# A decoder trunk whose hand-ordered mixer gets other starting points for its pairs of heads and other handicaps for its threads

## The chip, the cores and the metric

The kernel runs on one core of one Trainium2 chip. The metric is the device time of one execution in microseconds (us). Views of the profile speak of the engines as PE (TensorE's matmuls), PEld (TensorE loading the stationary operand), DVE (VectorE), ACT (ScalarE), POOL (GpSimd) and SP (SyncE, which here only issues transfers).

## The reference

Two layers run over one sequence of 256 positions with 1024 channels. Each layer does, in float32:

```
x = x + 0.5 * swiglu_ffn(x, ffn1)                 # 1024 -> 2 x 2816 -> 1024
h = rms_norm(x);  z = h @ w_in                    # columns shared out among all branches and gates
o_sb  = stick_breaking_attention(...)             # 8 heads of 64
o_mla = mla_attention(...)                        # 8 heads, low-rank q and kv, rotary part of 32
o_nsa = nsa_attention(...)                        # 8 heads, 2 kv groups: compressed, selected, window
y = sum over the 3 branches of sigmoid(gate_b(h)) * (o_b @ proj_b)
x = x + y @ w_out
x = x + 0.5 * swiglu_ffn(x, ffn2)
```

The part from `h` to `x + y @ w_out` is the mixer. Its three attentions are small (256 queries, 256 keys); nearly all its arithmetic is products with weights.

## The kernel before

**The weight stream.** All weights are read once, in the order of use, as slabs of 128 rows by (mostly) 1024 columns. Each float32 slab is split into a high part (a copy on ACT, L926 in the mixer, L527 in the FFNs) and a low part (a subtraction on DVE, L928, L528), and each product is three matmuls: high by high, low by high, high by low (`mm3`, L573 to L575). A slab of 1024 columns is so 12 matmuls of 512 columns over the two halves of the sequence. Some of the mixer's slabs are split ahead of time during an FFN and parked in HBM (`split_early`; `EARLY_AT` says which, the first tuple for both layers, the second for layer 1 alone). These come back as two finished halves (L914) and need no ACT and no DVE work, but twice the bytes.

**The mixer's slabs** are numbered 0 to 68: 0 to 3 low-rank inputs, gates and rotary key, 4 to 7 the queries of the stick-breaking attention (SB), 8 to 14 its keys together with the MLA up-projections, 15 to 18 its values, 19 to 22 queries and 23 to 26 keys of the sparse attention (NSA), 27 to 30 a merge gate, 31 and 32 values of NSA, 33 to 34 the projection of SB, then gates and projections by turns with the compression weights of NSA at 39, 40 and 44, 45; 49, 50 and 55, 56 are the projection of MLA, 57 to 64 NSA's two merge gates, 65 to 68 NSA's projection, which needs the outputs of NSA's pairs of heads.

**The planner.** In the mixer the orders of PE, ACT and DVE are written out by a planner in the program: every strand of work is a generator (a thread) that yields one step at a time with its engine, its estimated duration, what it waits for and which buffers it needs. At each turn the planner issues the step with the lowest rank,

```
s = self.start(req[0], req[3], req[4])
rank = s + (th[0]() if callable(th[0]) else th[0]) + (0.5 * req[1] if isinstance(th[2], list) else 0.0)
```

where `s` is the earliest start by its own estimates in us and `th[0]` is the thread's handicap, `HOLDS`. The threads in the order of `HOLDS` are `hT_rest, tables, sb_T, sb_scores, sb_pv, cmp_in, nsa_prep, gates, mla_T, mla_scores, mla_P, mla_pv, nsa_T, k_chain, v_chain, cmp_scores, nsa_scores, nsa_P, nsa_pv, bulk`. `bulk` (handicap 0.3) is the weight products, slab after slab, which fill the time between the others. The thread that splits the weights has a handicap that depends on its lead over the slab in use (`URGENCY`: no slab of lead, one, two and more). The engines then run these orders as they stand: where a step is ready later than the planner estimated, its engine stands at it, whatever stands behind.

**The pairs.** Heads are worked on in pairs, four in each attention. A pair's first step waits for a gate, the end of a given slab:

```
def gate(at, p, ahead=0):
    return ev_used[max(0, at[p] + ahead)]
```

For SB the pair's transposes (L1353) wait for slab `SB_AT[p] - 2` and its scores (L1368, L1374) for `SB_AT[p]`; for MLA the same with `MLA_AT` (transposes L1521, scores at lines 573 to 575 into `att`); for NSA the scores (L1845) of pair `p` wait for slab `NSA_AT[2 * p]`, and the odd entries are not read. After the scores, `t_softmax` runs minima (DVE L1462), exponentials (ACT L1452), a reciprocal and a scaling (ACT L1484 or DVE L1482); `t_probs` transposes the result on PE (L1493) and splits it (ACT L944 or DVE L946, DVE L1501); PE multiplies by the values (MLA L1333 to L1339; NSA L1868 to L1871 twice for a pair and L1878, L1879 for the compressed branch); `put_o` adds two halves and splits the sum (ACT L1312, DVE L1318, ACT L952, DVE L954). SB has a longer chain in `sb_head` (L1382 to L1412, with two PE steps L1401, L1402 in the middle). Buffers that two pairs share: four `qk` tiles (a pair of SB takes two, of MLA all four, until its scores are done), four banks for scores (an SB or MLA pair takes two, an NSA pair all four), four `wf` and four `wr` tiles.

**The one transfer inside the mixer that PE waits for** is `zc`: POOL sends two tiles from `wf` to `zc` (L1216), and `cmp_in` transposes them (L1613).

Of the kernel before, what the change touches and what calls it, by code (L numbers as in the profile page):

```python
# [242 lines left out]
class Planner:  # L243
# [11 lines left out]
    def spawn(self, gen, hold=0.0):  # L255
        try:
            self.live.append([hold, gen, next(gen)])
        except StopIteration:
            pass
# [74 lines left out]
def use_t(count, *deps, slots=()):  # L334

    o = 0.2 + count * 0.109
    return "P", o, o + 0.2, deps, slots
# [15 lines left out]
TAIL = 3  # L353

MIX_SLABS = 69
SB_AT = 19, 21, 23, 26
MLA_AT = 30, 33, 36, 39

EARLY_AT = tuple(range(27, 47, 2)), tuple(range(28, 48, 2))

URGENCY = (-1.0, -0.3, 0.15)
HOLDS = (0.0, 2.0, 0.0, 0.0, 0.0, 0.05, 0.05, 0.05, 0.05, 0.05, 0.05, 0.05, 0.05, 0.05, 0.05, 0.0, 0.05, 0.05, 0.05, 0.3)
NSA_AT = 46, 48, 50, 52, 54, 56, 58, 60


@with_exitstack
def decoder_trunk(ctx, tc, x_in, wts, gains, lcon, cst, out, depth=DEPTH):
# [15 lines left out]
    def tp_tile():  # L383
        return pb.tile([128, 512], F, tag="ps", name="tp")
# [156 lines left out]
    def split_early(fp, l, part):  # L541

        for a in EARLY_AT[part]:
            i = l * len(plan) + FFN_SLABS + a
# [293 lines left out]
    def mixer(l):  # L838
# [98 lines left out]
        def urgency():  # L937
            return URGENCY[min(loading[0] - use_at[0], 2)]

# [408 lines left out]
        def sb_T():  # L1348
            for p in range(4):
                k = yield use_t(4, *ev_sbqk[0], *ev_sbqk[1], gate(SB_AT, p, -2), slots=(s_tp, s_qk, s_qk))  # L1350
                tp = tp_tile()
# [10 lines left out]
        def sb_scores():  # L1362
            for p in range(4):
                k = yield "P", 1.0, 1.2, (ev_qsb[p], gate(SB_AT, p)), (s_att, s_att)
                q = qsb[p]
# [70 lines left out]
        def gate(at, p, ahead=0):  # L1436

            return ev_used[max(0, at[p] + ahead)]
# [73 lines left out]
        def mla_T():  # L1512
            for p in range(4):
                T = []
                for i, (src, ev) in enumerate(((mq, ev_mq), (mk, ev_mk))):
                    k = yield use_t(4, *ev, gate(MLA_AT, p, -2), slots=(s_tp, s_qk, s_qk))
                    tp = tp_tile()
# [14 lines left out]
        def mla_scores():  # L1532
            for p in range(4):
                k = yield "P", 1.44, 1.64, (*ev_Tm[p], gate(MLA_AT, p), ev_tanh), (s_att, s_att)
                T = Tm[p]
                s = [att_tile() for _ in range(2)]
                r = slice(0, 96)
                for j in range(2):
                    o = 256 * j
                    mm3(s[j][:, 0:128], cut(T[0], r, slice(o, o + 128)), cut(T[1], r, slice(o, o + 128)),  # L1540
                        start=True, stop=True)
                    mm3(s[j][:, 128:384], cut(T[0], r, slice(o + 128, o + 256)), cut(T[1], r, slice(o, o + 256)),
                        start=True, stop=True)
                s_qk.put(k, k, k, k)
                sb = [(x[:, 0:128], x[:, 128:384]) for x in s]
                spawn(t_softmax(sb, 1.0 / math.sqrt(96.0), None, k, 0.01 * p, Em[p], ev_Em[p]), 0.01 * p)

        def mla_P():
            for p in range(4):
                yield from t_probs(Em[p], ev_Em[p], Pm[p], ev_Pm[p], 0.01 * p)  # L1550

        def mla_pv():
            for p in range(4):
                k = yield *PV, (*ev_Pm[p], *ev_V1), (s_acc,)
                oT = acc_tile()
                pv(oT, V1, (2 * p, 2 * p + 1), [[q[:, j] for q in Pm[p]] for j in range(2)])
                s_wr.put(k, k)
                spawn(put_o(o_mla, p, oT, k, ev_omla), 0.01 * p)
# [204 lines left out]
        def v_chain():  # L1763

            k = yield use_p(64, 3, ev_hidT[1], slots=(s_acc,))
            a = acc_tile()
            mm3(a[:, 0:64], flat(hvs[1]), cut(tab["w2"], A, slice(64, 128)), start=True, stop=True)
            vs = mp.tile([128, 2, 64], R, name="vc")
            k = yield from t_split(vs[:, 0], vs[:, 1], a[:, 0:64], 64, k)
            s_acc.put(k)  # L1770
            k = yield use_v(1024, k)
            nc.vector.tensor_tensor(Vc, bc(vs.rearrange("p a d -> p (a d)"), 8),
                                    cc("vm")[:, :, None].to_broadcast([128, 8, 128]), op=OP.mult)
            ev_vc.set(k)
# [59 lines left out]
        def nsa_scores():  # L1834

            for p in range(4):
                k = yield "P", 1.3, 1.5, (*ev_nT, ev_sg, ev_cs, gate(NSA_AT, 2 * p)), (s_att,) * 4
                g = p // 2
                s = [[att_tile() for _ in range(2)] for _ in range(2)]
                for t in range(2):  # L1840
                    q, w = slice(128 * t, 128 * t + 128), 128 * (t + 1)
                    for i, (x, y_) in enumerate(((0, 0), (0, 1), (1, 0))):
                        for j in range(2):
                            r = slice(64 * j, 64 * j + 64)
                            nc.tensor.matmul(s[j][t][:, 0:2 * w].rearrange("p (b k) -> p b k", b=2),  # L1845
                                             nq[x][r, p, q], nk[y_][r, g, :, 0:t + 1, :].rearrange("p b c k -> p b (c k)"),
                                             start=i == 0, stop=i == 2)
                left = [2, 2]
                for b in range(2):
                    u = 2 * p + b  # L1850
                    gt = sg[:, :, 1 + b, 2 * p:2 * p + 2].rearrange("p t h -> p h t")
                    sb = [[s[j][t][:, 128 * (t + 1) * b:128 * (t + 1) * (b + 1)] for t in range(2)] for j in range(2)]
                    spawn(t_softmax(sb, 0.125, gt, k, 0.01 * u, En[u], ev_En[u], left), 0.01 * u)

        def nsa_P():
            for u in range(8):
                yield from t_probs(En[u], ev_En[u], Pn[u], ev_Pn[u], 0.01 * u)
# [37 lines left out]
        for th, hold in zip((hT_rest(), tables(), sb_T(), sb_scores(), sb_pv(), cmp_in(), nsa_prep(), gates(), mla_T(),  # L1895
                             mla_scores(), mla_P(), mla_pv(), nsa_T(), k_chain(), v_chain(), cmp_scores(), nsa_scores(),
                             nsa_P(), nsa_pv(), bulk()), HOLDS):
            spawn(th, hold)
# [55 lines left out]
```

## Time and profile before

| | |
|---|---|
| median of 3 runs | 1296.68 us (1296.1 to 1299.27) |
| profiled execution, its own time | 1296.9 us |
| its span, first to last instruction | 1295.1 us |
| busy share of the span: PE, PEld, DVE, ACT, POOL | 99%, 82%, 69%, 61%, 8% |
| mixer of layer 0, of layer 1 | about 197 to 435 us, 839 to 1076 us |

The 1.8 us between the profiled execution's own time and its span lie before and behind the instructions. Matmul ends are modelled in the profile and overlap the next matmul's start, so the busy share of PE says less than the distance between the starts of two matmuls.

### The profile page before, as it was taken

To read this page: it belongs to the slowest core of one execution; us is meant where nothing else is said; L and a number is where in the kernel's file an instruction comes from. 1 tells how busy PE (TensorE), PEld (TensorE's weight loads), DVE (VectorE), ACT (ScalarE), POOL (GpSimd) and SP (SyncE) were. 2 spreads that over 40 slices of the span, in tenths; PEclk is the share of its full clock that TensorE was granted. 3 is DMA by queue.
4 is the path that set the end of the run, shared out by engine and by line. 5 is a ranking of instruction groups with operands and counts; after the bars stand their busy time and mean duration, and the time that the engine had idled before them with its cause. 6 is when DMAs were issued, how large, how long until landed. Compare 5 with 4: busy or idle time off the path is not lost.

```text
span 1295.1 us, 19900 instructions
## 1 busy us (share of the span) xinstructions
PE 1278.8 (99%) x6335; PEld 1056.7 (82%) x6335; DVE 894.0 (69%) x1880; ACT 790.6 (61%) x1646; POOL 107.8 (8%) x170
## 2 busy tenths in 40 slices
PE   8999999999999999999999999999999999999998
PEld 6888888888877888888888888888888778888887
DVE  6666667978788676665577765679767876755553
ACT  6555557787777566554466654478766874645442
POOL 0111000210000011110011210011100000000000
PEclk9999999999999999999999999999999999999999
DMA  7898876655645569987669996575687355555563
GB/s 245 313 316 303 278 260 218 190 179 192 203 136 163 170 204 352 325 306 237 194 219 352 354 323 198 177 234 174 222 269 250 122 171 179 179 184 190 180 193 116
DMA packets 151387, 293.71 MB, mean 227 GB/s; under 512 B 17768, under 2 KB 19440, under 8 KB 151280
## 3 DMA queue, kind: packets, MB, share of 16 engines
q1 hardware_dynamic: 141424, 260.43, 62.1%
q0 software_dynamic: 9856, 31.99, 6.3%
q8 instruction: 50, 0.82, 0.3%
q14 instruction: 57, 0.47, 0.1%
HBM read 257.22 MB, written 34.60 MB: 225 GB/s over the span
## 4 chain that ended last, share of the span: by engine, by line
PE 84%; DVE 8%; ACT 5%; issue 2%; DMA 1%; POOL 0%; SPq 0%; DVEq 0%; ACTq 0%; POOLq 0%
PE acc L573 26%; PE acc L575 26%; PE acc L574 25%; DVE wlo L928 2%; PE tp L725 1%; ACT wf L1452 1%; ACT whi L926 1%; DVE wr L1501 1%; ACT wf L1484 1%; DVE x L669 1%; PE tp L592 1%; DVE wf L1462 1%; PE att L1402 0%; PE tp L1493 0%; DVE wlo L528 0%
## 5 line engine op out<-in xcount | busy, mean ns | idle before, releaser
L528 DVE TENSOR_TENSOR wlo<-raw,whi 128x512 fp32r<-128x512 f32 (+1 forms) x560 | 360.5, 685 | 197.2 <-ACT whi L527 196.1
L573 PE MATMUL acc<-whi,hThi 128*128 128x512 f32 (+2 forms) x1184 | 468.5, 396 | 0.0
L527 ACT ACTIVATE whi<-raw 128x512 fp32r<-128x512 f32 (+1 forms) x560 | 322.2, 622 | 231.2 <-PE acc L575 204.5
L575 PE MATMUL acc<-whi,hTlo 128*128 128x512 f32 (+2 forms) x1184 | 459.1, 388 | 0.0
L574 PE MATMUL acc<-wlo,hThi 128*128 128x512 f32 (+2 forms) x1184 | 458.3, 387 | 0.0
L575 PEld LDWEIGHTS acc<-whi,hTlo 128*128 128x128 f32 x1184 | 222.9, 188 | 45.8
L573 PEld LDWEIGHTS acc<-whi,hThi 128*128 128x128 f32 x1184 | 223.2, 189 | 41.3 <-issue 1.1
L574 PEld LDWEIGHTS acc<-wlo,hThi 128*128 128x128 f32 x1184 | 223.5, 189 | 39.8
L928 DVE TENSOR_TENSOR wlo<-raw,whi 128x512 fp32r<-128x512 f32 x216 | 141.1, 678 | 35.0 <-ACT whi L926 31.4
L926 ACT ACTIVATE whi<-raw 128x512 fp32r<-128x512 f32 x216 | 126.4, 617 | 43.3 <-PE acc L575 35.7
L573 PE MATMUL acc<-whi,gh 128*128 128x512 f32 x352 | 138.3, 393 | 0.0
L575 PE MATMUL acc<-whi,gl 128*128 128x512 f32 x352 | 137.2, 390 | 0.0
L574 PE MATMUL acc<-wlo,gh 128*128 128x512 f32 x352 | 137.0, 389 | 0.0
L555 DVE TENSOR_TENSOR elo<-eraw,ehi 128x512 fp32r<-128x512 f32 x60 | 41.4, 690 | 78.3 <-ACT ehi L554 77.9
L554 ACT ACTIVATE ehi<-eraw 128x512 fp32r<-128x512 f32 x60 | 37.9, 631 | 94.4 <-DMA eraw<-in_wts 90.7
L580 POOL TENSOR_TENSOR rs<-ss,mh 128x1 f32<-128x1 f32 (+4 forms) x30 | 36.1, 1205 | 629.4 <-DVE ss L579 608.1
L575 PEld LDWEIGHTS acc<-whi,gl 128*128 128x128 f32 x352 | 66.1, 188 | 13.8
L574 PEld LDWEIGHTS acc<-wlo,gh 128*128 128x128 f32 x352 | 66.2, 188 | 13.3
L573 PEld LDWEIGHTS acc<-whi,gh 128*128 128x128 f32 x352 | 66.1, 188 | 13.3
L556 POOL DMA_DIRECT2D early<-ehi x60 | 32.7, 545 | 294.7 <-ACT ehi L554 277.2
L1452 ACT ACTIVATE wf<-wf,mn 128x128 f32<-128x128 f32 x96 | 42.5, 445 | 15.2 <-DVE mn L1462 15.1
L573 PE MATMUL acc<-whi,oh 128*128 128x512 f32 x96 | 39.3, 409 | 0.0
(277 smaller groups left out, 1385.9 us busy)
## 6 DMA issues: line engine op xcount, KB each, us to landing
raw<-in_wts SPq DMA_DIRECT2D x764, 256.0 KB, 3.3
eraw<-in_wts SPq DMA_DIRECT2D x60, 256.0 KB, 5.2
early<-ehi POOLq DMA_DIRECT2D x60, 256.0 KB, 4.3
early<-elo POOLq DMA_DIRECT2D x60, 256.0 KB, 4.9
whi<-early SPq DMA_DIRECT2D x60, 256.0 KB, 4.0
wlo<-early SPq DMA_DIRECT2D x60, 256.0 KB, 3.5
gain<-in_gains SPq DMA_DIRECT2D x5, 512.0 KB, 7.4
xd<-x SPq DMA_DIRECT2D x4, 512.0 KB, 4.4
```

Source lines behind the costliest of these rows:

```text
L527: nc.scalar.activation(hi[:, c:c + m], raw[:, :m], AF.Copy)
L528: nc.vector.tensor_tensor(lo[:, c:c + m], raw[:, :m], hi[:, c:c + m], op=OP.subtract)
L554: nc.scalar.activation(hi, raw, AF.Copy)
L555: nc.vector.tensor_tensor(lo, raw, hi, op=OP.subtract)
L556: nc.gpsimd.dma_start(d[0], hi.bitcast(F))
L573: nc.tensor.matmul(o, a[0], b[0], start=start, stop=False)
L574: nc.tensor.matmul(o, a[0], b[1], start=False, stop=False)
L575: nc.tensor.matmul(o, a[1], b[0], start=False, stop=stop)
L580: nc.gpsimd.tensor_tensor(r[:p, :w], ss[:p, :w], mh[:p, :w], op=OP.pow)
L926: nc.scalar.activation(hl[0][:, c:c + m], raw[:, :m], AF.Copy)
L928: nc.vector.tensor_tensor(hl[1][:, c:c + m], raw[:, :m], hl[0][:, c:c + m], op=OP.subtract)
L1452: nc.scalar.activation(E[i][:, cs], E[i][:, cs], AF.Exp, scale=-1.0, bias=mn[:, q:q + 1], accum_out=su[:, q:q + 1])
```

## The change

Only constants change. The second pair of SB begins one slab sooner and the third three slabs sooner; the second pair of MLA begins three slabs later and the third two later; of the entries of `NSA_AT` that are read (0, 2, 4, 6), the first goes from 46 to 45, the second stays at 50, the third goes from 54 to 57 and the fourth from 58 to 60. In layer 1 the slabs 26 and 48 are split ahead of time in place of 30 and 46. The thread of the weights gets other handicaps, and twelve of the twenty threads too.

```
-SB_AT = 19, 21, 23, 26
-MLA_AT = 30, 33, 36, 39
-
-EARLY_AT = tuple(range(27, 47, 2)), tuple(range(28, 48, 2))
-
-URGENCY = (-1.0, -0.3, 0.15)
-HOLDS = (0.0, 2.0, 0.0, 0.0, 0.0, 0.05, 0.05, 0.05, 0.05, 0.05, 0.05, 0.05, 0.05, 0.05, 0.05, 0.0, 0.05, 0.05, 0.05, 0.3)
-NSA_AT = 46, 48, 50, 52, 54, 56, 58, 60
+SB_AT = (19, 20, 20, 26)
+MLA_AT = (30, 36, 38, 39)
+
+EARLY_AT = ((27, 29, 31, 33, 35, 37, 39, 41, 43, 45), (28, 26, 32, 34, 36, 38, 40, 42, 44, 48))
+
+URGENCY = (-0.4, -0.6, 0.15)
+HOLDS = (0.0, 2.0, -0.2, -0.2, 0.1, -0.15, 0.05, 0.35, 0.25, 0.25, 0.05, 0.05, 0.05, 0.05, -0.35, 0.0, 0.25, 0.05, 0.25, 0.3)
+NSA_AT = (45, 47, 50, 54, 57, 59, 60, 61)
```

By thread: `sb_T` and `sb_scores` from 0 to -0.2, `sb_pv` from 0 to 0.1, `cmp_in` from 0.05 to -0.15, `gates` from 0.05 to 0.35, `mla_T`, `mla_scores`, `nsa_scores` and `nsa_pv` from 0.05 to 0.25, `v_chain` from 0.05 to -0.35; the others keep theirs.

## Rows read from the trace of the kernel before

**Rows 1.** The page: busy time, share of the span and instructions of each engine, and the granted clock of TensorE in tenths of full speed in 40 slices.
```profile
PE 1278.8 (99%) x6335; PEld 1056.7 (82%) x6335; DVE 894.0 (69%) x1880; ACT 790.6 (61%) x1646; POOL 107.8 (8%) x170
...
PEclk9999999999999999999999999999999999999999
```

**Rows 2.** Busy time by stretch of the whole mixers and of an FFN between them: stretch and its width in us, busy us (and instructions) of PE, PEld, DVE, ACT, POOL, then granted clock, DMA share and GB/s.
```profile
197.00:435.00 238.00, 234.96 (x1324) 194.12 (x1323) 194.14 (x500) 179.95 (x431) 17.69 (x15) 1.00 0.58 182
839.00:1076.00 237.00, 233.61 (x1324) 193.82 (x1324) 184.04 (x482) 169.98 (x409) 17.67 (x15) 1.00 0.64 205
480.00:640.00 160.00, 160.00 (x729) 132.37 (x727) 98.38 (x156) 86.88 (x156) 21.35 (x40) 1.00 0.86 290
```

**Rows 3.** The same view by stages of the mixer of layer 0.
```profile
230.00:260.00 30.00, 30.00 (x151) 24.65 (x151) 28.38 (x62) 23.60 (x47) 6.42 (x5) 1.00 0.60 177
260.00:290.00 30.00, 30.00 (x186) 25.64 (x183) 23.25 (x48) 24.47 (x54) 4.87 (x5) 1.00 0.56 175
290.00:320.00 30.00, 28.76 (x187) 24.90 (x185) 26.65 (x71) 24.35 (x60) 2.27 (x1) 1.00 0.59 186
320.00:350.00 30.00, 29.18 (x197) 24.75 (x196) 22.79 (x65) 21.58 (x57) 0.55 (x1) 1.00 0.60 209
350.00:380.00 30.00, 29.80 (x183) 23.57 (x181) 26.83 (x94) 22.82 (x69) 0.00 (x0) 1.00 0.49 150
380.00:410.00 30.00, 29.84 (x158) 22.51 (x157) 24.92 (x75) 23.57 (x62) 0.00 (x0) 1.00 0.46 138
410.00:435.00 25.00, 24.43 (x116) 19.43 (x115) 17.04 (x42) 16.12 (x37) 0.00 (x0) 1.00 0.56 190
```

**Rows 4.** What the loads of PE's stationary operand waited for, over the whole span, first at the transposes L1493, then at L1869: us in total, times.
```profile
  ACT wf L1484: 9.2, 19
...
  DVE wr L1501: 5.1, 11
```

**Rows 5.** PE in order of time in layer 0 around the last pair of NSA, at the start of slab 65 (428.56) and at the first product that reads the output of that last pair (431.96, in slab 66): start, duration, engine, line, operation; in brackets the idle time before it.
```profile
406.47 1.32 PE L1845 MATMUL att<-nk,nq 64*128 64x256 f32 x12
...
417.46 0.50 PE L1868 MATMUL acc<-wr,V 128*128 128x512 f32 x1
418.49 0.45 PE L1869 MATMUL acc<-wr,V 128*64 128x512 f32 x1 [0.53 <-DVE wr L1501]
...
428.56 0.39 PE L573 MATMUL acc<-whi,oh 128*128 128x512 f32 x1
428.79 0.39 PE L574 MATMUL acc<-wlo,oh 128*128 128x512 f32 x1
...
431.96 0.39 PE L573 MATMUL acc<-whi,oh 128*128 128x512 f32 x1
```

**Rows 6.** DVE in the same stretch: the last splitting of that pair's output.
```profile
421.87 0.42 DVE L954 TENSOR_TENSOR ol<-of,oh 128x256 fp32r<-128x256 f32 x1
```

**Rows 7.** PE around the first transposes of the first pair of MLA and of the fourth (layer 0).
```profile
306.95 0.33 PE L1493 MATMUL tp<-ident,wf 128*128 128x128 f32 x1
308.19 0.44 PE L1493 MATMUL tp<-ident,wf 128*128 128x128 f32 x2 [0.91 <-ACT wf L1484]
...
342.54 1.13 PE L1493 MATMUL tp<-ident,wf 128*128 128x128 f32 x5 [0.67 <-ACT wf L1484]
```

**Rows 8.** The chain of work that ends at 308.83 us, in order of time: start, duration, engine, tile, line.
```profile
305.18 0.60 DVE qk L954
...
306.90 0.48 ACT qk L952
...
307.74 1.09 ACT wf L1484 x3
```

**Rows 9.** PE at the largest wait for ACT in layer 1's NSA stage.
```profile
1024.67 0.44 PE L1493 MATMUL tp<-ident,wf 128*128 128x128 f32 x2 [0.48 <-ACT wf L1484]
```

**Rows 10.** The transfer `zc`: POOL's issuing of it in both layers (ns, least, median, most; first and last start), its time to landing, SP's issuing of parked slabs beside it in layer 1, and PE's wait there.
```profile
L1216 POOL DMA_DIRECT2D zc<-wf x8: 618/630/688, 281.3 to 925.5; - x8
...
DMA to landing us min/median/max: 2.0/3.3/4.5
...
924.69 3.12 SPq L914 DMA_DIRECT2D wlo<-early  x2
...
929.66 0.63 PE L1613 MATMUL tp<-ident,zc 128*128 128x128 f32 x4 [1.30 <-DMA zc<-wf]
```

**Rows 11.** DVE's groups in 320 to 350 us of layer 0: instructions, busy us, mean ns of one.
```profile
L928 DVE TENSOR_TENSOR wlo<-raw,whi 128x512 fp32r<-128x512 f32 x9 | 6.1, 685 | 1.4 <-ACT whi L926 1.4
L1501 DVE TENSOR_TENSOR wr<-tp,wr 128x384 fp32r<-128x384 f32 x6 | 3.2, 549 | 0.4 <-ACT wr L944 0.3
...
L1462 DVE CUSTOM_DVE_ANT_0 wf<-att,ct 128x128 f32<-128x128 f32 (+1 forms) x8 | 2.4, 351 | 0.0
L954 DVE TENSOR_TENSOR qk<-tp,qk 96x512 fp32r<-96x512 f32 x3 | 2.1, 687 | 1.8 <-ACT qk L952 1.7
```

**Rows 12.** PE at the scores of other pairs in layer 0, in order of time: MLA's third and NSA's first.
```profile
323.91 0.23 PE L573 MATMUL att<-qk 96*128 96x128 f32 x1
...
359.13 1.32 PE L1845 MATMUL att<-nk,nq 64*128 64x256 f32 x12
```

**Rows 13.** PE at NSA's second pair in layer 0: the start of its scores and its last product with values.
```profile
370.57 0.62 PE L1845 MATMUL att<-nk,nq 64*128 64x256 f32 x6
...
387.20 0.28 PE L1871 MATMUL acc<-wr,V 128*128 128x256 f32 x1
```

## The prediction

> **What bounds the kernel now.** First the page: PE is busy for 1278.8 of 1295.1 us, at full granted clock (2.4 GHz) in every slice, while no other engine passes 69% [rows 1]. So time is won or lost only where PE's order stands still. Busy time by stretch, next, shows where that is: the FFN stretch has no idle time (160.00 of 160.00 us), the mixers have 238.00 - 234.96 = 3.04 us in layer 0 and 237.00 - 233.61 = 3.39 us in layer 1 [rows 2], together 6.4. That is too little, since a matmul's modelled end covers the beginning of a wait: in order of time L1868 and L1869 start 418.49 - 417.46 = 1.03 us apart, two matmuls of that width usually 428.79 - 428.56 = 0.23 us [rows 5]. So 0.80 us are lost there and 0.53 shown, 0.27 hidden. The loads of the stationary operand see all waits: 9.2 us in 19 at the transposes L1493 and 5.1 in 11 at L1869 [rows 4], but some of that time PE is still at the matmul before. The truth lies between 6.4 and 14.3 us; with half of the 0.27 hidden at each of 30 waits it is 6.4 + 4.1, so I take 10.5 us. It is the ceiling of what another order can win (1286.4 us by the profiled execution's 1296.9). Nothing bounds a loss from above.
>
> The waits lie where probabilities come back to PE: the transposes wait for ACT's scaling, the product with values for DVE's low half. The idle times in the rows name ACT's scaling, DVE's low half and one transfer [rows 5, 7, 9, 10]; none names the splitting of weights.
>
> **The change part by part.** No arithmetic is added or removed; PE, ACT, DVE and the transfers have the same steps, but for which two slabs come back parked.
>
> *Handicap of the products with values (nsa_pv, 0.05 to 0.25).* Against bulk's 0.3 the planner accepted up to 0.25 us of planned standing before such a product and now accepts 0.05. Real lateness comes on top of what is planned, so up to 0.20 us goes at each of the 11 waits: 0 to 2.2 us. The work put in its place is a step of the weight stream, three matmuls of 0.23 us [rows 5], which is there until slab 65. I take -1.5.
>
> *MLA's second pair, three slabs later.* Its transposes now wait for slab 34 in place of 31, so the splitting of its `qk` tiles leaves the stretch before 308 us. The chain shows it straight ahead of the scaling that the first pair's transposes wait for: 0.60 us on DVE at 305.18 and 0.48 us on ACT at 306.90 [rows 8]. PE stands there 308.19 - 306.95 = 1.24 us less one transpose [rows 7], 1.1 us lost; the pair's other head has a set of transposes too. Between nothing and 2.2 us (the same twice); I take -1.4, the 1.08 of the chain and part of the other head.
>
> *MLA's second and third pair now fall close to the fourth.* Gates 36, 38 and 39 put the starts at about 324, 332 and 335 us (the third began at 323.91 when gate 36 opened [rows 12]); the fourth must wait for the `qk` tiles of the third and slips. DVE in 320 to 350 us is busy 22.79 of 30 us [rows 3]; a pair brings four minima at 0.351, two tile splits at 0.687 and two low halves at 0.549 [rows 11], 1.4 + 1.4 + 1.1 = 3.9 us before its output is put together, so about 27 of 30. The wait at 342.54 (0.67 idle [rows 7]) then grows. Below: nothing, since weights can be split ahead in the emptier stage before; above: it doubles and comes twice more, +3. I take +1.0. What MLA delivers is used only from slab 49, over 15 us later; NSA's transposes wait for MLA's last ones and are late next, but NSA's first pair starts at 359.13 [rows 12] behind a chain through the compression that doesn't pass here.
>
> *NSA's third and fourth pair, three and two slabs later.* Two slabs are 24 matmuls, 24 x 0.227 = 5.4 us (0.227 is (431.96 - 428.56) / 15 [rows 5]). The fourth pair's output is whole at 421.87 + 0.42 = 422.29 [rows 6] and first read at 431.96 [rows 5]; 9.7 us of cover become 4.2. I take 0. If the pair were as slow as the second, whose scores and last product lie 387.20 - 370.57 = 16.6 us apart [rows 13] against 418.49 - 406.47 = 12.0 [rows 5], the cover would be gone (4.2 - 4.6) and the cost 0.4 a layer. The stage it goes to has DVE at 17.04 of 25 us, the one it leaves 24.92 of 30 [rows 3].
>
> *SB's second and third pair sooner.* PE has no idle time in 230 to 290 us (30.00 twice [rows 3]), so nothing can be won. DVE is at 28.38 of 30 before 260 and 23.25 after: the third pair can't pass the four banks for scores that the first two hold, so less moves than the gates say. I take 0; if a weight half is pushed behind, 0.685 us each [rows 11], above: +1.
>
> *Parked slabs 26 and 48 for 30 and 46, layer 1.* Slab 48 parked takes 2 x 0.685 us from DVE [rows 11] in the stage of the wait at 1024.67 (0.48 idle [rows 9]); slab 46 gives them back some 5 us sooner. 0 to -1.0; I take -0.4. Slab 30 now loads raw, half the bytes and two transfers fewer, while `zc` is on its way. In layer 1 PE waits 1.30 us for `zc`; SP's issuing beside it shows 3.12 us for two parked halves, and the slowest landing was 4.5 us against 2.0 for the fastest [rows 10]. -1.3 to 0; I take -0.7.
>
> The Trainium skill (SBUF — State Buffer, SBUF: two separate sides) has another cause for such a landing: DVE in a two-port mode locks GpSimd out, and it can't write the descriptors of its own transfer, whatever SP does. By that rule `zc` would stay late and the sum be 0.7 us higher. The trace speaks rather against it, since POOL's issuing takes 618 to 688 ns in both layers [rows 10].
>
> *Handicaps of cmp_in (-0.15) and v_chain (-0.35).* Both are now taken up to 0.2 and 0.4 us before they are ready, in two layers: 0 to +1.2, I take +0.3. The weights' thread is less urgent without lead and more with one slab; as PE waits for no slab now, 0; if one half comes late, +0.685 [rows 11]. The rest (gates, `mla_T`, scores) moves steps by 0.2 to 0.3 us behind the weight stream: 0.
>
> Sum: -1.5 - 1.4 + 1.0 - 0.4 - 0.7 + 0.3 = -2.7 us. On the profiled execution's own 1296.9 that is 1294.2; the median of the runs is 0.2 below it, so 1294.0 us.
>
> **The rivals.**
>
> *The waits only change places.* They arise where a step is later than the planner estimated, and its estimates aren't changed; the same 48 sets of transposes meet other backlogs. For it: 19 of them wait now [rows 4], in every stage; some gates don't bind (NSA's first pair starts behind other work). Against: the chain at 308 us names work that really leaves. It would give 1296.5, between 1296.2 and 1298.2.
>
> *A larger gain.* The waits at L1869 go altogether, MLA's pairs meet no crowd: the sum with the far bounds, -2.2 - 2.2 - 1.0 - 1.3 = -6.7, gives 1290.0 us.
>
> *NSA's last pair too late (slower).* From 410 us two pairs overlap, with PE's pure weight products shrinking to slabs 61 to 64. It decides from the point where a pair takes 4.2 us longer from scores to output than now. At 8 us longer, PE stands 4 us at slab 66 in each layer: 1296.7 + 8 = 1304.7. For it: the second pair, at DVE 26.83 of 30 us [rows 3], took 4.6 us longer. Against: the new stage's DVE is busy for 0.68 of the time, the old one's for 0.83 [rows 3].
>
> *MLA's crowd outweighs* what is won: +3 there and half the gains, 1296.7 + 3 - 2 + 0.3 = 1298.0, up to 1300.
>
> *The parked slabs don't help `zc`* (the rule above): 1294.7, a chance of 1 in 4, held within the forecast.
>
> **How the numbers follow.** Forecast (-0.5 to -5.5 us) 48%, places only 22%, larger gain 15%, NSA's tail 8%, MLA's crowd 7%. Within 0.3% means 3.9 us, about what a measurement of this kernel can tell. Faster by more: the larger gain and the far part of the forecast, 15 + 20 = 35%. Slower by more: the tail and the far end of the crowd, 8 + 3 = 11%. The same: 54%. The range leaves out the tail, a third of the larger gain and the crowd's end: 1288.5 to 1300.0 us.
>
> **What would show it.** Right: PE's idle time in the mixers falls from 6.4 to about 4.5 us; L1869's 5.1 us of load waits shrink by half; no transposes wait over 0.5 us near 305 to 316 us; a wait over 0.7 us appears between 335 and 355; `zc` in layer 1 costs under 1 us; PE runs into slab 66 without a stop. Wrong: PE idle at the first products of NSA's projection (tail); 19 or more waits at L1493 with 9 us (places only); weight products that wait for DVE L928 (urgency); SB's stage with idle PE.

## Result and the profile after

The changed kernel takes 1288.72 us (median of 6 runs, 1287.5 to 1290.04) against 1296.58 of the kernel before (6 runs): ratio 0.9936, 95% interval 0.9926 to 0.9946, so 7.9 us faster. The forecast was 1294.0 with 1288.5 to 1300.0. The direction held and the time is inside the range, but the gain is three times the sum of 2.7 us. The profiled execution's own time is 1288.63 us. The page, lines that answer to [rows 1]:

```profile
PE 1273.8 (99%) x6335; PEld 1056.7 (82%) x6335; DVE 897.5 (70%) x1886; ACT 789.0 (61%) x1640; POOL 107.2 (8%) x170
...
PEclk9999999999999999999999999999999999999999
```

PE has the same 6335 instructions. Six steps that either of two engines can do went from ACT to DVE (three scalings, L1484 to L1482, and three splits, L944 to L946), where the prediction had each engine's steps unchanged. Busy time by stretch of the two mixers, columns as in [rows 2]:

```profile
196.00:431.00 235.00, 232.62 (x1324) 194.01 (x1322) 196.50 (x506) 177.98 (x424) 17.40 (x15) 1.00 0.59 185
835.00:1067.00 232.00, 231.04 (x1321) 193.63 (x1320) 184.46 (x481) 169.20 (x409) 17.36 (x15) 1.00 0.66 210
```

PE is idle for 235.00 - 232.62 = 2.38 us in layer 0 and 0.96 in layer 1, together 3.3 where it was 6.4 [rows 2]. From the first transposes of the input (L995) to the first of the output (L1890) layer 0's mixer takes 232.32 us (before 235.26) and layer 1's 229.77 (before 234.34), 7.5 us less together. The FFN between them and the tail behind stay within 0.3 us (406.47 to 406.21, 215.26 both). The mixer of layer 0 begins at 198.78 and began at 199.62; that start lay between 198.8 and 200.7 over all the profiled executions below, so single lengths of a mixer tell more here than a single span.

What PE still waits for, from 190 to 1100 us (us in total, times, longest):

```profile
PE tp L1613 <- DMA zc<-wf: 1.5, 1, 1.5
PE tp L1493 <- ACT wf L1484: 1.1, 3, 0.6
PE acc L573 <- DVE hvl L954: 0.5, 1, 0.5
```

And what the loads of the stationary operand waited for, first at L1493, then at L1869, which answers to [rows 4]:

```profile
  ACT wf L1484: 3.9, 9
  DVE wf L1482: 0.9, 4
...
  DVE wr L1501: 1.5, 5
```

The waits for ACT's scaling went from 9.2 us in 19 to 3.9 in 9, those for DVE's low half from 5.1 in 11 to 1.5 in 5.

Idle time hides the first part of a wait. So for the runs below a second measure is used, which no view has: in PE's order of time the distance from each matmul of the mixers to the next, less what that kind and width usually takes; surpluses over 0.13 us are added up by the line that waited. It gives, in us:

```
          L1493   L1868/L1869   L1613 (zc)    others   sum
before     5.6       2.6        1.4 layer 1     1.4    11.0
after      2.3       0          1.6 layer 0     1.6     5.5
```

So 5.5 of the 7.5 us are waits over 0.13 us; the other 2.0 are smaller surpluses, whose places weren't separated. By this measure the ceiling worked out in the prediction, 10.5 us, was about right, though surpluses under 0.13 us lie outside it; more than half was won, not a quarter.

### The profile page after: what moved, and what is told of

It is laid out like the page before. It is cut to its first block, busy times and chain, and to the rows that moved or that the text cites. A ratio compares the mean times of both kernels' runs of the same rounds, so it can differ in the third digit from the quotient of the medians.

```text
span 1286.8 us, 19919 instructions
## 1 busy us (share of the span) xinstructions
PE 1273.8 (99%) x6335; PEld 1056.7 (82%) x6335; DVE 897.5 (70%) x1886; ACT 789.0 (61%) x1640; POOL 107.2 (8%) x170
## 4 chain that ended last, share of the span: by engine, by line
PE 92%; DVE 3%; ACT 2%; DMA 1%; issue 1%; SPq 0%; POOL 0%; DVEq 0%; ACTq 0%
PE acc L573 28%; PE acc L575 27%; PE acc L574 27%; PE tp L725 1%; PE tp L1493 1%; DVE x L669 1%; ACT wf L1452 1%; PE tp L592 1%; PE att L1845 1%; DVE wlo L928 1%; PE att L1402 1%; DMA raw<-in_wts 1%; PE tp L1521 0%; PE att L1374 0%; DVE wlo L528 0%
```

## Experiments

In the diffs the entries of `HOLDS` stand by the thread that they belong to; ten of the twenty differ, those that the section on the change lists, not twelve. All medians are in us, the ratio is to the kernel before on the same chip at the same time. Differences in the text are between medians: for parts added, against the kernel before measured beside them (1296.90 to 1297.39), for parts taken back, against after's 1288.72; by the ratios they come out up to 1.3 us apart. The table holds what the texts below refer to: waits by the measure above, the time after a wait in which TensorE's granted clock was half (1.2 GHz), and the lengths of the two mixers, all from the one profiled execution.

```
                 median  ratio [95%]               L1493 L1868/69 L1613  half  layer 0  layer 1
before          1296.58  1                          5.6    2.6    1.4    0     235.26   234.34
after           1288.72  0.9936 [0.9926, 0.9946]    2.3    0      1.6    0     232.32   229.77
added to the kernel before
pv_only         1296.16  0.9981 [0.9972, 0.9991]    5.5    1.3    2.1    3.4   234.26   235.18
handicaps_only  1295.52  0.9984 [0.9976, 0.9993]    3.4    1.3    2.9    6.8   232.73   236.80
gates_only      1299.21  1.0012 [1.0003, 1.0021]    2.3    4.2    4.0    3.4   234.16   237.65
early_only      1295.35  0.9984 [0.9975, 0.9993]    4.8    3.8    0      0     235.14   233.09
three_only      1292.53  0.9965 [0.9951, 0.9978]    4.5    1.9    0      0     233.63   231.77
jitter          1294.10  0.9978 [0.9969, 0.9988]    3.9    1.6    3.4    3.4   234.06   235.08
taken back from the kernel after
early_back      1293.65  0.9970 [0.9958, 0.9982]    1.5    0.8    4.3    3.4   231.07   235.60
park30          1293.78  0.9974 [0.9963, 0.9985]    2.3    0.2    5.0    0     231.98   233.59
pv_back         1291.46  0.9952 [0.9939, 0.9965]    2.3    2.8    1.1    0     233.48   230.73
mla_back        1289.27  0.9935 [0.9920, 0.9950]    2.2    0.8    1.6    0     232.29   230.23
nsa_back        1293.32  0.9966 [0.9955, 0.9978]    3.4    1.1    1.4    0     233.88   231.64
sb_back         1289.07  0.9938 [0.9925, 0.9950]    2.9    0      0      0     230.91   231.11
gates_back      1292.60  0.9959 [0.9945, 0.9973]    4.2    1.7    0      0     232.72   232.82
nsa_third       1293.94  0.9975 [0.9966, 0.9984]    3.9    2.2    2.4    3.4   236.45   231.91
new values in the kernel after
better          1289.59  0.9940 [0.9927, 0.9953]    0.7    1.6    0.3    0     231.72   230.12
better2         1295.81  0.9983 [0.9974, 0.9992]    7.5    0.8    0.9    3.4   237.60   231.00
zc_estimate     1287.99  0.9923 [0.9910, 0.9936]    2.3    0      0      0     230.61   229.62
```

`cmp_late` stands by itself below. In better2 3.9 of the 7.5 us is one wait for DVE's `su`.

### Parts added to the kernel before

**pv_only**: the handicap of the products with values alone.

```diff
-HOLDS nsa_pv  0.05
+HOLDS nsa_pv  0.25
```

> The kernel before with one number changed: the handicap of nsa_pv from 0.05 to 0.25. Theory H by the prediction's term: 1.5 us faster (0 to 2.2), load waits at L1869 from 5.1 to about 2.5 us, the waits at L1493 unchanged. Theories G and L: within 1 us of before.

The load waits at L1869 fell from 5.1 us in 11 to 2.5 in 7, and the surplus before them from 2.6 to 1.3 us, as the step has it. One run doesn't show that it is the step, since jitter below, with nsa_pv at 0.05, has 2.0 us in 6. But the other four at 0.05 (before, early_only, gates_only, pv_back) have 5.1 to 7.9 us, and all fifteen at 0.25 have 1.5 to 3.5. The time fell by 1.2 us by the medians, 2.5 by the ratio. More was lost again: in layer 1 PE was idle for 2.0 us for `zc` and ran at half clock for 3.4 us behind that wait.

**handicaps_only**, **gates_only**: the two halves of the change without the parked slabs.

```diff
-HOLDS, URGENCY of the kernel before
+HOLDS, URGENCY of the changed kernel
```
```diff
-SB_AT, MLA_AT, NSA_AT of the kernel before
+SB_AT, MLA_AT, NSA_AT of the changed kernel
```

> The kernel before with the new HOLDS and URGENCY alone; gates and parked slabs as before. Theory H (the handicaps take planned standing out of PE's order): most of the 7.9 us gained, 4 to 7 us faster than before, load waits at L1869 down from 5.1 us to under 2.5 us. Theory G (the pairs' new starting points do it): at most 2 us faster, L1869 still near 4 to 5 us. Theory L (any new order falls out within some us, this one well): anything from 3 us faster to 3 us slower, without relation to the parts.

> The kernel before with the new SB_AT, MLA_AT and NSA_AT alone; handicaps, urgency and parked slabs as before. Theory H: at most 2 us faster, load waits at L1869 still 4 to 5 us. Theory G: 4 to 7 us faster, load waits at L1493 down from 10 us to about 5. Theory L: as in the run with the handicaps alone.

-1.9 and +1.8 us: the sum is nothing, and neither half alone makes the gain. Both take waits away at L1493, the gates alone add some at L1869 (7.9 us of load waits in 15), and both have a later `zc` in layer 1, 2.7 us idle in handicaps_only (with the gates 3.4 by the surplus). Stretch, width, busy time of PE, PEld, DVE, ACT and POOL, clock, DMA share and GB/s, in handicaps_only behind that wait:

```profile
927.20:933.00 5.80, 5.79 (x19) 5.22 (x20) 2.23 (x5) 0.49 (x1) 0.00 (x0) 0.50 0.24 89
```

The clock is 0.50 where every stretch in [rows 2, 3] has 1.00. Not every execution has such a stretch: three of the twelve of handicaps_only show a mean granted clock of 1.000 and take 1292.97 to 1293.40 us, the profiled one 0.997 and 1296.17. So the -1.9 probably holds a gain of about 4 us that most executions lose in part behind `zc`.

**jitter**: no part of the change, eight handicaps moved by 0.02 us.

```diff
-HOLDS hT_rest, sb_T, sb_scores, nsa_prep, mla_P, nsa_T, nsa_P, bulk  0.0, 0.0, 0.0, 0.05, 0.05, 0.05, 0.05, 0.3
+HOLDS hT_rest, sb_T, sb_scores, nsa_prep, mla_P, nsa_T, nsa_P, bulk  0.02, 0.02, 0.02, 0.07, 0.07, 0.07, 0.07, 0.32
```

> The kernel before with handicaps shifted by 0.02 us (hT_rest, sb_T, sb_scores, nsa_prep, mla_P, nsa_P, nsa_T, bulk), too little to mean anything, but enough to make another order. Theories H and G: within 1 us of before. Theory L: 2 us or more away from it on either side.

A move that means nothing makes the kernel about 3 us faster (ratio 0.9978), as much as this change's forecast. A part that is worth under about 3 us by itself can't be told here, by its time alone, from the planner's choosing another order. Nor is one wait that goes where a step said it would enough: in jitter the load waits at L1869 fall as well, and the wait before MLA's first pair at 308 us goes. What counts is a wait that comes and goes with one part over several runs.

**early_only** and **three_only**: the parked slabs alone, and together with NSA's gates and nsa_pv.

```diff
-(28, 30, 32, 34, 36, 38, 40, 42, 44, 46)
+(28, 26, 32, 34, 36, 38, 40, 42, 44, 48)
```
```diff
-NSA_AT = (46, 48, 50, 52, 54, 56, 58, 60)
+NSA_AT = (45, 47, 50, 54, 57, 59, 60, 61)
-HOLDS nsa_pv  0.05
+HOLDS nsa_pv  0.25
```

> The kernel before with the new EARLY_AT alone (slabs 26 and 48 parked in layer 1 in place of 30 and 46). Theory Z (a parked slab's four transfers, issued by SP just ahead of zc, make zc late in layer 1): PE's wait at L1613 in layer 1 falls from 1.46 us between matmul starts to under 0.3, the rest stays, 1 to 2 us faster. The rival by the lock between DVE and POOL: the wait stays at 1 to 3 us, time within 0.7 us of before. Theory L: anything within 3 us, with or without the wait.

> The kernel before with three of the parts alone: the new EARLY_AT, the new NSA_AT and the handicap of nsa_pv at 0.25. If these three carry the gain: 1287.5 to 1290, no wait for zc over 0.5 us in layer 1, load waits at L1869 under 3 us, the third NSA pair shorter by some 4 us. If the other handicaps, SB and MLA are needed too: 1291 or more. If the other handicaps cost time (the parts undone add up to 5 us too much): under 1287.

The slabs alone take the wait for `zc` away in layer 1 (1.4 to 0) and give 1.6 us. The three parts give 4.5 us, a bit over half. The rest needs the other handicaps, SB's and MLA's gates.

### The parked slabs taken back

**early_back**, **park30**: the old slabs in the changed kernel, then slab 30 alone.

```diff
-(28, 26, 32, 34, 36, 38, 40, 42, 44, 48)
+(28, 30, 32, 34, 36, 38, 40, 42, 44, 46)
```
```diff
-(28, 26, 32, 34, 36, 38, 40, 42, 44, 48)
+(28, 30, 32, 34, 36, 38, 40, 42, 44, 48)
```

> The changed kernel with the old EARLY_AT. Theory Z: layer 1 waits 2 to 3.5 us for zc, as in the runs with the handicaps or the gates alone (2.9 and 3.4), so 2 to 3.5 us slower than the changed kernel: 1290.7 to 1292.3. The rival by the lock: no wait in layer 1, as in the changed kernel, time within 0.7 us of it.

> The changed kernel with slab 30 parked in layer 1 again in place of 26, while 48 stays parked and 46 not. Theory Z (the parked slab that SP issues beside zc): the wait for zc in layer 1 comes back with 3 us or more and a stretch of half granted clock behind it, 3.5 to 5 us slower than the changed kernel, 1292 to 1294. If it was the swap of 46 and 48: within 1 us of the changed kernel.

+4.9 and +5.1 us (4.6 and 3.5 by the mixers), the first more than expected: it is slab 30 alone, and what 46 or 48 does can't be seen. In order of time, early_back in layer 1 (start, duration, engine, line; first SP's issuing of the parked slab, then POOL's of `zc`, then PE):

```profile
918.02 0.32 SPq L914 DMA_DIRECT2D wlo<-early  x1
918.44 0.93 SPq L914 DMA_DIRECT2D whi<-early  x2
919.41 0.45 SPq L914 DMA_DIRECT2D wlo<-early  x1
...
917.67 1.32 POOL L1216 DMA_DIRECT2D zc<-wf  x2 [30.30 <-ACT wf L1214]
919.27 1.23 POOL L1216 DMA_DIRECT2D zc<-wf  x2 [0.29 <-ACT wf L1214]
...
921.97 0.39 PE L575 MATMUL acc<-whi,hTlo 128*128 128x512 f32 x1
926.02 1.08 PE L1613 MATMUL tp<-ident,zc 128*128 128x128 f32 x4 [3.67 <-DMA zc<-wf]
926.75 0.77 PE L573 MATMUL acc<-whi,hThi 128*128 128x512 f32 x1
927.33 0.63 PE L574 MATMUL acc<-wlo,hThi 128*128 128x512 f32 x1
927.75 0.63 PE L575 MATMUL acc<-whi,hTlo 128*128 128x512 f32 x1
928.18 0.63 PE L573 MATMUL acc<-whi,hThi 128*128 128x512 f32 x1
```

And the kernel after, the same places:

```profile
916.94 0.84 SPq L914 DMA_DIRECT2D whi<-early  x2
917.88 0.38 SPq L914 DMA_DIRECT2D wlo<-early  x1
...
918.88 1.32 POOL L1216 DMA_DIRECT2D zc<-wf  x2 [30.25 <-ACT wf L1214]
920.48 1.23 POOL L1216 DMA_DIRECT2D zc<-wf  x2 [0.28 <-ACT wf L1214]
...
923.40 0.60 PE L1613 MATMUL tp<-ident,zc 128*128 128x128 f32 x4
923.76 0.48 PE L573 MATMUL acc<-whi,hThi 128*128 128x512 f32 x1
924.08 0.39 PE L574 MATMUL acc<-wlo,hThi 128*128 128x512 f32 x1
```

In both POOL issues `zc` in 1.32 and 1.23 us, and PE's order comes to the transposes 1.7 us after POOL is done. With slab 30 parked SP issues four transfers of 256 KB while POOL issues `zc`, and PE waits until 926.02; with slab 30 raw SP's last issue of a parked slab ends 0.6 us ahead of POOL's first, and PE doesn't wait. All runs split in this way in layer 1. In the seven with slab 30 parked four of SP's issues fall among POOL's, the last transfer of `zc` lands 4.0 to 6.0 us after its issue began, and PE loses 1.5 to 3.8 us. In the thirteen with it raw none falls there, the last lands in 1.9 to 2.5 us, and PE loses at most 0.4. What the 16 DMA engines do in the five microseconds around POOL's issuing, early_back and then after (last two columns DMA share and GB/s):

```profile
917.00:922.00 5.00, 5.00 (x32) 4.00 (x30) 1.60 (x3) 4.84 (x11) 4.03 (x5) 1.00 0.95 309
```
```profile
918.00:923.00 5.00, 5.00 (x32) 4.04 (x31) 1.39 (x3) 4.76 (x11) 3.82 (x5) 1.00 0.66 236
```

So `zc` shares full DMA engines in one and emptier ones in the other. The Trainium skill (DMA: Bandwidth & Descriptors, Issuing engines are not separate DMA queues) says that transfers from SP and POOL run on the same 16 engines and interleave, whichever engine issued them; the trace is in line with it, 0.95 against 0.66 with a wait of 3.7 against none.

In early_back the matmuls behind the wait start 0.43 us apart, others 0.227, and the four transposes take 0.73 us for after's 0.36: about 1.5 us more until 929.3. With the wait's 3.8 that is 5.3 of the 5.8 us by which layer 1 is longer than after's. In park30 a wait of 3.5 us had no such stretch behind it.

### The other parts taken back

**pv_back**, **mla_back**, **nsa_back**, **sb_back**, **gates_back**, each from the changed kernel:

```diff
-HOLDS nsa_pv  0.25
+HOLDS nsa_pv  0.05
```
```diff
-MLA_AT = (30, 36, 38, 39)
+MLA_AT = (30, 33, 36, 39)
```
```diff
-NSA_AT = (45, 47, 50, 54, 57, 59, 60, 61)
+NSA_AT = (46, 48, 50, 52, 54, 56, 58, 60)
```
```diff
-SB_AT = (19, 20, 20, 26)
+SB_AT = (19, 21, 23, 26)
```

gates_back has the last three at once.

> The changed kernel with the handicap of nsa_pv back at 0.05. Theory H (planned standing ahead of the products with values): load waits at L1869 back from 1.5 us to between 4 and 8 (7.9 in the run with the gates alone), 1.5 to 3 us slower than the changed kernel, 1290.2 to 1291.7. Theory G: within 1 us of the changed kernel.

+2.7 us. The load waits at L1869 are back, 6.0 us in 12, and the surplus there 2.8 us: the whole difference.

> The changed kernel with the old MLA_AT. Theory M (the second MLA pair's tile splits delay the first pair's scaling): transposes L1493 wait 1 to 2 us between 300 and 318 us of layer 0 again, 1 to 2.5 us slower than the changed kernel, 1289.7 to 1291.2. By the prediction's term for the crowd at 324 to 345 us its going should win 1.0 back, so that both together give 1289 to 1290.5. Theory L: within 3 us on either side, waits elsewhere.

+0.5 us, within the intervals. In layer 0 PE has the very same order with either gates, so they don't bind there. In layer 1 they do: the second pair's first scores come 113.1 us into the mixer, for 117.9 after, and layer 1 takes 0.46 us longer. What moved MLA in layer 0 is another step. ACT loads its table for the exponential (L1433) ahead of MLA's first scores; of before, after and mla_back:

```profile
299.07 1.28 ACT L1433 ACT_TABLE_LOAD   x1
```
```profile
305.43 1.28 ACT L1433 ACT_TABLE_LOAD   x1
```
```profile
307.04 1.28 ACT L1433 ACT_TABLE_LOAD   x1
```

Counted from the mixer's start that is 99.4, 106.7 and 106.6 us. The first pair's scores come at 100.3, 111.1 and 111.0. With the handicaps alone (handicaps_only) the table comes at 105.2, with the gates alone at 100.1. So it is the order that the new handicaps give which holds MLA back, by 10.8 us for the first pair and 4.8 to 9.2 for the others, and not the gates. Nor need it be the size of the handicaps, since in jitter the table comes at 105.1.

> The changed kernel with the old NSA_AT. The prediction's term was 0: within 1 us of the changed kernel. Theory S (the two last NSA pairs, set three and two slabs later, meet an emptier DVE and ACT): the waits behind 370 us and 1010 us at L1493 and L1869 come back, 1 to 3 us slower, 1289.7 to 1291.7. Theory L: within 3 us on either side.

+4.6 us by the medians, more than either theory's 3, 3.9 by the ratios, 233.88 - 232.32 + 231.64 - 229.77 = 3.4 us by the mixers; the profiled execution's mixer began 1.65 us later than after's, which is within what that start varies. By position it is the third pair that differs. From its first score to its last product with values it takes 11.4 us in after and 15.4 before and 16.1 here (layer 0). DVE within that time of before, then of after (line, tiles, count | busy us, mean ns):

```profile
L928 DVE TENSOR_TENSOR wlo<-raw,whi 128x512 fp32r<-128x512 f32 x8 | 5.4, 686 | 1.2 <-PE att L1845 1.2
...
L1272 DVE TENSOR_TENSOR y<-y,th 128x512 f32<-128x512 f32 x2 | 1.4, 686 | 0.0
L1269 DVE SCALAR_TENSOR_TENSOR th<-th,acc 128x512 f32<-128x512 f32 x2 | 1.4, 684 | 0.1
```
```profile
L928 DVE TENSOR_TENSOR wlo<-raw,whi 128x512 fp32r<-128x512 f32 x7 | 4.6, 688 | 0.5 <-ACT whi L926 0.5
```

Before, two merges of MLA's output (L1269, L1272, 2.8 us of DVE) fall into the third pair; after, the pair begins behind them (the last ends at 395.78, the scores start at 396.05) and one weight split fewer falls in. Behind 363 us no wait over 0.13 us is left in layer 0 up to slab 66, and nsa_back has 2.1 us of them there. The runs split alike in both layers: with the merges within it the third pair takes 15.4 to 17.5 us (seven runs), without them 11.4 (twelve runs). The one left, nsa_third below, has no merges there and takes 14.8. So the merges go with the length; that they cause it, and the loss of time with it, is argued and not shown by itself.

> The changed kernel with the old SB_AT. The prediction's term was 0: within 1 us of the changed kernel, no wait over 0.3 us at the SB steps (L1374, L1401, L1402) in either. Theory L: within 3 us on either side, because everything behind it is ordered anew.

+0.35 us: no difference in the whole. But layer 0 takes 1.41 us less than after's and layer 1 1.34 more. In this run PE doesn't wait for `zc` in either layer. SP's last issue ahead of POOL's first of `zc` in layer 0, after and then sb_back:

```profile
279.84 0.38 SPq L513 DMA_DIRECT2D raw<-in_wts  x1
...
280.38 1.33 POOL L1216 DMA_DIRECT2D zc<-wf  x2 [30.30 <-ACT wf L1214]
```
```profile
280.60 0.38 SPq L914 DMA_DIRECT2D wlo<-early  x1
...
282.31 1.33 POOL L1216 DMA_DIRECT2D zc<-wf  x2 [30.27 <-ACT wf L1214]
```

In the twelve runs with the new SB_AT SP's last issue ends about 0.15 us ahead of POOL's first, and the last transfer of `zc` lands in 2.5 to 4.3 us; in the eight with the old it ends 1.25 to 1.33 us ahead, and the last lands in 2.0. PE waits in layer 0 in ten of the twelve (not in cmp_late and zc_estimate, where it comes later) and in none of the eight. So SB's new gates bring the wait for `zc` in layer 0. What they win back in layer 1 isn't placed.

> The changed kernel with the old SB_AT, MLA_AT and NSA_AT: handicaps, urgency and parking are new. NSA's gates back alone cost 4.6 us, SB's and MLA's 0.4 and 0.5. If the gates' worth is NSA's third and fourth pair: 1292.5 to 1294. If the three sets only fit together: above 1294.5. If any set would do once zc is on time: within 1.5 us of the changed kernel.

+3.9 us, no more than NSA's gates alone: SB's and MLA's add nothing to the whole, as two runs now say.

**nsa_third**: the third pair at its new gate, the fourth (and the first) at its old.

```diff
-NSA_AT = (45, 47, 50, 54, 57, 59, 60, 61)
+NSA_AT = (46, 48, 50, 52, 57, 59, 58, 60)
```

> The changed kernel with NSA's gates at 46, 50, 57, 58: of the new gates only the third pair's is kept. If the gain hangs on the third pair's place behind MLA's last merges: within 1.5 us of the changed kernel, 1287.2 to 1290.2. If the fourth pair's later gate is needed: the fourth pair meets the third, waits at L1493 and L1869 behind 405 us of layer 0 come back and the time is 1290.5 to 1293.3.

+5.2 us, above both ranges. In the profiled execution, the longest of the ten, layer 0 takes 4.1 us more than after's, with `zc` 1.9 us late and half clock behind, and layer 1 2.1 more with `zc` hardly late (0.4). In both layers the fourth pair's scores come 4.2 us behind the third's, for 13.0 after, and the waits at L1493, L1868 and L1869 behind them are back, 1.4 us in each layer where after has none. So the third pair's gate alone doesn't give the gain; the fourth pair's later one is needed too. How much of the +5.2 is `zc` stays open.

### New values

**cmp_late**: a later compression, to see what `cmp_in` is worth.

```diff
-HOLDS cmp_in  -0.15
+HOLDS cmp_in  1.5
```

> The changed kernel with the handicap of cmp_in at +1.5 us in place of -0.15, so that PE puts more weight products ahead of the transposes of zc. Theory Z: the 1.6 us wait at L1613 in layer 0 of the changed kernel goes, nothing else does: 1 to 1.6 us faster than the changed kernel, 1287.1 to 1287.7. Theory L: within 3 us on either side, the wait gone or not.

1311.63 us, ratio 1.0109 [1.0091, 1.0127]. It told neither theory from the other. A handicap of 1.5 lies above bulk's 0.3, so the planner takes this step only when no weight product can run, and PE came to stand for it. TensorE ran at half clock for 13.7 us in layer 0 and 10.2 in layer 1. Two of the waits:

```profile
PE acc L1650 <- DVE zw L954: 4.4, 2, 2.2
PE tp L1493 <- DVE wf L1482: 3.4, 2, 2.0
```

**better**, **better2**: more threads at 0.25, then `cmp_in` and `v_chain` alone.

```diff
-HOLDS cmp_in, mla_P, mla_pv, v_chain, nsa_P  -0.15, 0.05, 0.05, -0.35, 0.05
+HOLDS cmp_in, mla_P, mla_pv, v_chain, nsa_P   0.25, 0.25, 0.25, 0.25, 0.25
```
```diff
-HOLDS cmp_in, v_chain  -0.15, -0.35
+HOLDS cmp_in, v_chain   0.25, 0.05
```

> The changed kernel with the handicaps of cmp_in, v_chain, mla_P, nsa_P and mla_pv all at 0.25, just under bulk's 0.3 (before: -0.15, -0.35, 0.05, 0.05, 0.05). Theory H: planned standing goes at these steps too; the waits at L1613 (1.6), behind the v chain (0.6) and at L1493 (2.3) shrink by half or more, 2 to 3 us faster than the changed kernel, 1285.7 to 1286.7. Theory L: within 3 us on either side.

> The changed kernel with cmp_in at 0.25 (from -0.15) and v_chain at 0.05 (from -0.35). Theory H: the wait for zc in layer 0 (1.6) and the one behind the v chain (0.6) go, 1 to 2 us faster than the changed kernel, 1286.7 to 1287.7. Theory L: within 3 us on either side.

better takes 1.6 us of the waits at L1493 away and 1.3 at `zc`, and new ones come: 1.6 at L1868 and L1869, 1.0 at L1680, and

```profile
PE acc L1878 <- DVE Vc L1772: 0.8, 1, 0.8
```

+0.9 us, where 2 to 3 us less was expected, and not told apart from the kernel after. In better2 a single set of transposes meets a backlog of DVE at 369.61 (3.94 idle for `su`), with half clock behind: +7.1 us. There the waits only changed places, the prediction's first rival.

**zc_estimate**: the planner's own number for when `zc` lands, nothing else.

```diff
-            z = Tok(k2.t + 3.0)
+            z = Tok(k2.t + 4.5)
```

> The changed kernel, with the planner's estimate for zc's transfer at 4.5 us after the copy in place of 3.0; the chip's transfer is the same. Theory Z: the transposes of zc come 1.5 us later behind more weight products, the 1.6 us wait in layer 0 goes, 1 to 1.6 us faster than the changed kernel, 1287.1 to 1287.7. Theory L: everything behind is ordered anew, 3 us faster to 5 us slower, as better2 was 7 slower.

1287.99 us, the lowest median of all, by 0.7 us (1.7 by the ratios). The wait is gone though the last transfer of `zc` lands in 3.4 us for 3.8 after; layer 0 takes 1.7 us less (230.61) and layer 1 0.15. The intervals overlap, so that the whole kernel is faster than after is likely, not shown.

## Why the prediction was right in direction and wrong in size

Two terms failed most. NSA's third and fourth pair stood at 0 and were worth 3.4 to 4.6 us when taken back, since the step priced only the place they go to. Parking, slab 30 above all, stood at -0.7 and at most -1.3 and was worth 3.5 to 5.1 when taken back, since the step took the old order's wait as the most that can be won. The sum also took the parts to add, and they don't. That the time fell inside the range owes something to the range's width.

- **Handicap of nsa_pv, -1.5.** Right in place, somewhat small. The surplus before L1868 and L1869 fell from 2.6 us to 0; without it 2.8 us are back and 2.7 of time. The upper bound of 2.2, 0.20 at each of the 11 waits, was too low: the waits didn't stay and shrink, most went altogether.
- **MLA's second pair later, -1.4.** The wait went (1.13 us at 308 us and 0.84 at 342.54 by the surplus, [rows 7]; after, the largest at MLA's transposes in layer 0 is 0.47), but not by the gates. The step read the gates as binding; the old ones give the same order in layer 0. The order that the handicaps give brings the table load 7.2 us later and the first pair 10.8, and with jitter, which has none of them, that wait goes too.
- **MLA's crowd, +1.0.** Wrong. With all pairs later and 8 to 12 us apart (10 to 14 before), no wait over 0.7 us comes between 335 and 355 us.
- **NSA's third and fourth pair, 0.** The largest miss of the sum that can be placed. The cover came out as worked out: the last pair's output is whole at 423.75 + 0.42 = 424.17 and first read at 428.18, 4.0 us later, where 4.2 was forecast. PE runs into slab 66 without a stop:

```profile
423.75 0.42 DVE L954 TENSOR_TENSOR ol<-of,oh 128x256 fp32r<-128x256 f32 x1
...
427.95 0.39 PE L575 MATMUL acc<-whi,ol 128*128 128x512 f32 x1
428.18 0.39 PE L573 MATMUL acc<-whi,oh 128*128 128x512 f32 x1
```

  But the step looked only at what could be lost behind the pair, and not at what the pair itself meets at its old place: at 395.85 to 400 us DVE merges MLA's output. That was in the trace of before. Undone, these gates cost 3.4 to 4.6 us, and nsa_third shows that the two belong together.
- **SB, 0.** The number came out (0.35), the reasoning didn't: the zero is 1.41 us lost in layer 0, where PE now stands for `zc` in SB's stage, against 1.34 won in layer 1. That the two cancel is luck. The step asked what SB's gates do to PE and DVE, and not to SP's issuing.
- **Parked slabs, -1.1.** The mechanism for slab 30 was right: SP's issuing beside POOL's makes `zc` late. The size was not. The sum took the wait of the trace before, 1.30 us [rows 10], as all that can be won. The 3.12 us read there as SP's issuing of two halves are two issues under 0.5 us with a pause between. In the new order PE comes to the transposes 1.7 us after POOL is done, for 2.1 before, `zc` lands in up to 6.0 us, and the wait would be 3.8 us with half clock behind; the term is worth 1.6 alone and 4.9 in company. Of slab 48 for 46, -0.4, nothing can be seen.
- **The rule on the shared port** (the Trainium skill, SBUF — State Buffer, SBUF: two separate sides). It did not decide here: POOL issues `zc` in 618 to 688 ns in after, early_back and park30 alike, whether the transfer lands in 2.1 us or in 6.3, and the wait comes and goes with SP's issuing. What is late after the change is `zc` in layer 0, where PE didn't wait before: 1.46 us idle, 1.6 by the surplus. That goes with SB's gates and SP's issuing (sb_back). Why the wait is 0.3 in early_back with the very same order of PE stays open.

```profile
284.68 0.39 PE L575 MATMUL acc<-whi,hTlo 128*128 128x512 f32 x1
286.53 0.63 PE L1613 MATMUL tp<-ident,zc 128*128 128x128 f32 x4 [1.46 <-DMA zc<-wf]
```

- **cmp_in and v_chain, +0.3.** Not measured by themselves; moving both the other way (better2) cost 7.1 us by one new wait.
- **The sum itself.** Taken back one at a time the parts are worth 2.7 + 0.5 + 4.6 + 0.35 + 4.9 = 13.1 us (10.5 by the ratios or the mixers), more than the 7.9 together; added one at a time to the kernel before, the handicaps, the gates and the slabs are worth 1.9, -1.8 and 1.6. The planner lays out everything anew after each edit, so the terms don't add. Such a sum can be expected to miss by some microseconds, as a move of 0.02 us in eight handicaps made about 3.

Of the signs named, idle time (3.3, forecast 4.5), L1869 (1.5, forecast half of 5.1), `zc` in layer 1 (none) and slab 66 came out or went further. No transposes wait over 0.5 us near 305 to 316 us either, but because MLA comes later. The new wait near 335 to 355 us did not come, and one sign of being wrong did: SB's stage with idle PE, 1.46 us at 286.53. Which of the other handicaps, or `URGENCY`, which never moved by itself, carry the remaining 3.4 us between three_only and after stays open.

## What to carry to other kernels

When pairs of steps are moved later, read what the engines do at the place that they leave and not only the cover at the place they go to: here a pair that starts behind another stage's merges, with the next pair far enough behind it, was a quarter shorter. A small transfer that a dense engine waits for should keep clear of a burst of large ones: here it landed late among SP's issues or 0.15 us behind them, and in time, or at most 0.4 us late, from 0.6 us on. A planner's estimate for it should be that of its loaded landing. In a kernel whose order a planner makes, price a part by taking it out of the finished kernel, measure what a meaningless move does first, and don't add such prices.

## What the runs showed of the hardware

- The 64 KB transfers of `zc` landed in 2.0 to 4.5 us before [rows 10] and in 3.5 to 6.3 with slab 30 parked in the new order (park30), with the same issuing time on POOL. In layer 0 the last of them landed in 2.0 us with 1.25 to 1.33 us between SP's last issue and POOL's first (eight runs), and in 2.5 to 4.3 us with about 0.15 (twelve).
- A wait of PE can cost more than its length. Behind seven waits (1.9 us in nsa_third, 2.0 in pv_only, 2.7 in handicaps_only, 3.1 in jitter, 3.3 in gates_only, 3.7 in early_back, 3.9 in better2) the granted clock was at its lower level, 1.2 GHz, for 3.4 to 6.8 us, and matmuls started 0.43 us apart for 0.227; behind the 1.3 us of before and the 1.5 of after it stayed at 2.4 in the profiled executions. Other executions of a kernel differ: of 33 of the kernel before the mean granted clock is 1.000 in one of 1295.57 us and 0.997 in one of 1300.61. It isn't the length alone: park30's wait of 3.5 us had none. The Trainium skill (TensorE: Matmul & The Clock Gate, Part 1: The HAM clock gate) has these two levels; the trace agrees, 0.50 and 1.00.
